# Row tiles and weight tiles loaded one by one at the start, and a new closing order, in a QKV projection on one core

## The chip, the cores and the metric

One core of a Trainium2 chip (trn2) runs the whole kernel. The metric is the device time of one execution in microseconds (us). A profiled execution has a **span**, from its first to its last recorded instruction, about 1.8 us shorter than that time.

## The reference, cut to what matters

```python
batch, seq, hidden = 16, 512, 768
x      # [16, 512, 768] float32
w_qkv  # [768, 2304]    float32

qkv = np.matmul(x, w_qkv)
q, k, v = qkv[..., :768], qkv[..., 768:1536], qkv[..., 1536:]
return np.stack([q, k, v], axis=0)
```

Flattened, x has 8192 rows, that is 64 row tiles of 128 rows or 32 pairs of row tiles.

## The kernel before

The first three pairs are multiplied plainly in bf16, against column blocks of 512, while the weights are still coming in. From pair 3 on a scheme with seven half-size products per pair is used. 256 "remainder" columns are always multiplied directly. A weight block of 512 columns comes as six k-tiles of 256 KB.

How row tiles are loaded, cast and turned (transposed by TensorE into PSUM, then copied out by the vector and scalar engines, half each):

```python
def load_rows(p):                       # one transfer for two row tiles, 768 KB
    xin[p] = xin_pool.tile([P, 2, K], fp32, name="xin")
    rows = x_flat[p * 2 * P:(p + 1) * 2 * P, :]
    nc.sync.dma_start(xin[p][:], rows.rearrange("(r m) k -> m r k", m=P))
# ... cast_rows(p): both tiles to bf16; turn_rows(p): six transposes each, copies
```

The order of the first loads, all on one queue, and of the first work:

```python
load_rows(0)
load_rows(1)
load_blocks(0, 0, 1)                    # six k-tiles, one transfer each
load_w(st_rem[:], 0, KT, R_OFF, REM)    # remainder columns
load_rows(2)
# ... more weights, more rows
busy(11)                                # filler matmuls on zeros
cast_rows(0); turn_rows(0)
busy(4)
cast_rows(1); cast_k(0); cast_k(1); turn_rows(1)
for j in range(2, KT): cast_k(j)
# ...
block(0, 0, b1[0], singles, nothing)    # four row tiles, k-tile by k-tile
rem(0); rem(1)                          # remainder columns of two pairs
cast_rows(2, False); turn_rows(2, False)
block(0, 0, b1[0], halves((4, 5)), nothing)
```

The closing order of the last pair (a and b are its two column halves, `do(u, n)` is product n with its eviction):

```python
do(a, 1); do(b, 1); do(a, 2); do(a, 6); do(b, 2); do(b, 6)
# ... stores, products 5 and 7
do(a, 4); rem_stored(0); do(b, 4)
do(a, 3); do(b, 3)
rem_stored(1)                           # remainder columns of the last row tile come last
```

## Time and profile before

| | before |
|---|---|
| time, median of the first 3 runs | 362.76 us |
| span of the profiled run | 361.4 us |
| TensorE busy | 353.3 us, 98% |
| first useful matmul | 9.19 us |
| first column block over six row tiles done | 20.54 us |
| last matmul to end of span | 4.53 us |

How to read it: the list of waits has no TensorE wait after 9 us, so only the start, the end and the work itself can move the time. The lines that carry this are in the prediction below.

### The profile page before, as it was taken

What the parts mean: (1) busy time and instruction counts of PE and PEld (TensorE: products, weight loads), DVE (VectorE), ACT (ScalarE), POOL (GpSimd) and SP (SyncE); (2) the same over time, 40 slices, a digit from 0 to 9 for tenths busy, and PEclk for the clock granted to TensorE, in tenths of its full rate; (3) what the DMA queues carried; (4) which work ended last, traced back from release to release, by engine and by line L of the source; (5) the groups of instructions that cost most, each with busy time, mean ns of one, the idle gap of its engine ahead of it and who ended that gap; (6) DMA issues with size and microseconds to landing.
All of it is one profiled execution on the core that took longest, in us unless ns stands there. A gap on an engine that the chain in (4) does not pass through costs nothing.

```text
span 361.4 us, 5220 instructions
## 1 busy us (share of the span) xinstructions
PE 353.3 (98%) x1765; PEld 250.8 (69%) x1797; DVE 222.7 (62%) x239; ACT 182.5 (51%) x304; POOL 174.4 (48%) x180
## 2 busy tenths in 40 slices
PE   8999999999999999999999999999999999999994
PEld 3644577777777777777777777777777777777763
DVE  3489546666566765566675565676556676556642
ACT  4547555455454545454545444445545454545452
POOL 0000970566664445664445665444666444566410
PEclk9999999999999999999999999999999999999999
DMA  7999969799899989999999999898999998989766
GB/s 294 381 383 338 348 227 345 271 354 304 279 322 298 296 275 296 282 313 314 284 278 295 282 306 316 284 276 291 295 285 317 295 296 276 297 279 331 267 251 242
DMA packets 80617, 108.08 MB, mean 299 GB/s; under 512 B 4816, under 2 KB 60368, under 8 KB 80592
## 3 DMA queue, kind: packets, MB, share of 16 engines
q1 hardware_dynamic: 65184, 96.35, 82.3%
q10 hardware_dynamic: 15408, 11.41, 9.9%
q8 instruction: 14, 0.23, 0.3%
q14 instruction: 11, 0.09, 0.1%
HBM read 32.24 MB, written 75.50 MB: 298 GB/s over the span
## 4 chain that ended last, share of the span: by engine, by line
PE 96%; ACT 1%; issue 1%; ACTq 0%; DVE 0%
PE ps L206 75%; PE ps L256 11%; PE ps L382 9%; PE ps L362 1%; PE ps L161 1%; ACT o L237 0%; ACTq L297 0%; ACT xb L141 0%; ACT orem L311 0%; DVE xb L139 0%; ACT xc L141 0%; ACTq L313 0%; DVE zero L340 0%; ACTq L311 0%
## 5 line engine op out<-in xcount | busy, mean ns | idle before, releaser
L206 PE MATMUL ps<-t,s 128*128 128x512 f32 x696 | 173.8, 398 | 0.0
L206 PEld LDWEIGHTS ps<-t,s 128*128 128x128 f32 x696 | 130.7, 188 | 29.8
L169 POOL CAST xb<-xf 128x1536 bf16<-128x1536 f32 x29 | 46.4, 1601 | 167.7 <-DVE xf L124 167.7
L234 DVE TENSOR_TENSOR o<-o,ps 128x512 f32<-128x512 f32 x58 | 39.9, 688 | 87.6 <-ACT o L233 87.6
L124 DVE STREAM_TRANSPOSE xf<-xin 128x1536 f32<-128x1536 f32 x29 | 85.7, 2956 | 9.7 <-DMA xin<-in_x_dram 7.1
L206 PE MATMUL ps<-b,xb 128*128 128x512 bf16 x320 | 82.4, 380 | 1.5
L233 ACT ACTIVATE o<-ps 128x512 f32<-128x512 f32 x58 | 34.7, 598 | 44.3 <-PE ps L206 44.3
L206 PEld LDWEIGHTS <-xb 128*128 128x128 bf16 x348 | 31.7, 98 | 35.6 <-issue 7.6
L227 ACT ACTIVATE o<-ps 128x512 f32<-128x512 f32 x58 | 34.8, 600 | 40.0 <-PE ps L206 37.3
L240 DVE TENSOR_TENSOR o<-o,ps 128x512 f32<-128x512 f32 x58 | 39.9, 688 | 21.4 <-PE ps L206 20.2
L206 PE MATMUL ps<-b,s 128*128 128x512 f32 x174 | 48.7, 389 | 0.0
L256 PE MATMUL ps<-w_rem,xb 128*128 128x256 bf16 x384 | 47.2, 273 | 0.0
L237 ACT ACTIVATE o<-ps 128x512 f32<-128x512 f32 x58 | 34.7, 598 | 24.1 <-PE ps L206 21.3
L220 ACT ACTIVATE o<-ps 128x512 f32<-128x512 f32 x58 | 34.6, 597 | 23.8 <-DVE o L240 20.7
L256 PEld LDWEIGHTS <-xb 128*128 128x128 bf16 x384 | 37.4, 98 | 11.2 <-issue 0.5
L224 DVE TENSOR_TENSOR o<-o,ps 128x512 f32<-128x512 f32 x58 | 36.5, 673 | 3.4 <-PE ps L206 2.1
L206 PEld LDWEIGHTS ps<-b,s 128*128 128x128 f32 x174 | 32.7, 188 | 6.8
L178 POOL TENSOR_TENSOR s<-s,xf 128x384 fp32r<-128x384 f32 x29 | 29.5, 1016 | 2.3
L266 ACT ACTIVATE orem<-ps 128x512 f32<-128x512 f32 x31 | 18.6, 598 | 22.7 <-PE ps L256 21.4
L179 POOL TENSOR_TENSOR s<-xf 128x384 fp32r<-128x384 f32 x29 | 29.5, 1017 | 0.0
L181 POOL TENSOR_TENSOR s<-xf,s 128x384 fp32r<-128x384 f32 x29 | 29.4, 1015 | 0.0
L177 POOL TENSOR_TENSOR s<-xf 128x384 fp32r<-128x384 f32 x29 | 29.3, 1012 | 0.0
(36 smaller groups left out, 127.2 us busy)
## 6 DMA issues: line engine op xcount, KB each, us to landing
out_dram<-o SPq DMA_DIRECT2D x62, 768.0 KB, 5.1
out_dram<-o SPq DMA_DIRECT2D x65, 256.0 KB, 4.6
xin<-in_x_dram SPq DMA_DIRECT2D x62, 192.0 KB, 6.7
xin<-in_x_dram ACTq DMA_DIRECT2D x54, 192.0 KB, 4.5
out_dram<-orem SPq DMA_DIRECT2D x31, 256.0 KB, 5.5
st<-in_w_qkv_dram SPq DMA_DIRECT2D x6, 768.0 KB, 14.1
xin<-in_x_dram SPq DMA_DIRECT2D x3, 768.0 KB, 5.8
st<-in_w_qkv_dram SPq DMA_DIRECT2D x6, 256.0 KB, 6.3
```

The source lines that it names most:

```text
L124: nc.vector.transpose(t[:].rearrange("p j (g b) -> p g j b", b=G), xin.pop(p)[:].rearrange("p g (a j) -> p g j a", a=G),)
L169: nc.gpsimd.tensor_copy(out=xb[p][:], in_=xf[p][:])
L206: nc.tensor.matmul(ps[:], lhs[j], rhs[j], start=(start and j == 0), stop=(j == KH - 1), skip_group_check=True,)
L220: nc.scalar.activation(c11, u.x[:], ident)
L224: nc.vector.tensor_tensor(c11, c11, u.z[:], op=add)
L227: nc.scalar.activation(c12, u.x[:], ident)
L233: nc.scalar.activation(c22, u.x[:], ident)
L234: nc.vector.tensor_tensor(c22, c22, u.y[:], op=add)
L237: nc.scalar.activation(c21, u.x[:], ident)
L240: nc.vector.tensor_tensor(c12, c12, u.y[:], op=add)
L256: nc.tensor.matmul(ps, xb[p][:, j, r * P:(r + 1) * P], w_rem[:, j, :], start=(j == 0), stop=(j == KT - 1), skip_group_check=True,)
L382: nc.tensor.matmul(ps[n][:], xb[p][:, j, r * P:(r + 1) * P], w[:, j, :], start=(j == 0), stop=(j == KT - 1), skip_group_check=True,)
```

## The change

Its intent is to start useful matmuls earlier and to shorten the end. The first loads come as row tiles 0, 1 and 2, k-tiles 0 to 4, row tile 3, k-tile 5; each row tile is a transfer of 384 KB. Three row tiles start on the k-tiles as they land, the fourth joins at the end. In the last pair the remainder columns go ahead of b's last two products, and the last eviction is cut in two halves.

```diff
-    def load_rows(p):
-        ...
-        nc.sync.dma_start(xin[p][:], rows.rearrange("(r m) k -> m r k", m=P))
+    def load_row(p, r):
+        if r == 0:
+            xin[p] = xin_pool.tile([P, 2, K], fp32, name="xin")
+        row = (2 * p + r) * P
+        nc.sync.dma_start(xin[p][:, r, :], x_flat[row:row + P, :])
 ... (cast_row and turn_row: likewise one tile at a time)
-    load_rows(0)
-    load_rows(1)
-    load_blocks(0, 0, 1)
+    load_row(0, 0)
+    load_row(0, 1)
+    load_row(1, 0)
+    for j in range(KT - 1):
+        load_k(j)
+    load_row(1, 1)
+    load_k(KT - 1)
 ... (remainder columns and pair 2: two transfers each in place of one)
-    busy(11)
-    cast_rows(0)
-    turn_rows(0)
-    busy(4)
-    cast_rows(1)
-    ...
+    busy(8)
+    cast_row(0, 0)
+    cast_row(0, 1)
+    turn_row(0, 0)
+    busy(1)
+    cast_row(1, 0)
+    turn_row(0, 1)
+    cast_k(0)
+    turn_row(1, 0)
 ... (block: k-tiles 0 to 4 for three tiles, fourth tile turned, k-tile 5, fourth tile)
-        do(a, 4); rem_stored(0); do(b, 4); do(a, 3); do(b, 3); rem_stored(1)
+        do(a, 4); do(a, 3); rem_stored(0); rem_stored(1); do(b, 4)
+        product(b, 3, b.y, False)        # evicted and stored in two halves of 256 columns
```

(The last two lines are condensed; the stores between them are left out.)

More of the change, by code (lines that the diff above doesn't have):

```diff
@@ L128, in transpose @@
         xf[p] = t
-    def load_rows(p):
-        xin[p] = xin_pool.tile([P, 2, K], fp32, name="xin")
-        rows = x_flat[p * 2 * P:(p + 1) * 2 * P, :]
-        nc.sync.dma_start(xin[p][:], rows.rearrange("(r m) k -> m r k", m=P))
+    def load_row(p, r):
[3 more added lines that the diff above has]
+        nc.sync.dma_start(xin[p][:, r, :], x_flat[row:row + P, :])
     def copy_halves(dst, src, two):
@@ L145, with cast_row, turn_row @@
     xc = {}
-    def cast_rows(p, two=True):
-        src = xin.pop(p)
-        xc[p] = s_pool.tile([P, 2, K], bf16, name="xc", tag="s")
-        for r in range(2):
-            halves = (slice(0, K // 2), slice(K // 2, K))
-            copy_halves([xc[p][:, r, n] for n in halves], [src[:, r, n] for n in halves], two)
-    def turn_rows(p, two=True):
-        c = xc.pop(p)
-        xb[p] = xb_pool.tile([P, KT, 2 * P], bf16, name="xb")
-        for r in range(2):
-            cols = c[:, r, :].rearrange("m (p j) -> m j p", j=KT)
-            ps = ps_pool.tile([P, KT, P], bf16, name="ps")
-            for j in range(KT):
-                nc.tensor.transpose(ps[:, j, :], cols[:, j, :], eye)
-            ks = (slice(0, KH), slice(KH, KT))
-            copy_halves(
-                [xb[p][:, n, r * P:(r + 1) * P] for n in ks], [ps[:, n, :] for n in ks], two
-            )
+    def cast_row(p, r, two=True):
+        if r == 0:
+            xc[p] = s_pool.tile([P, 2, K], bf16, name="xc", tag="s")
+        halves = (slice(0, K // 2), slice(K // 2, K))
+        copy_halves([xc[p][:, r, n] for n in halves], [xin[p][:, r, n] for n in halves], two)
+    def turn_row(p, r, two=True):
+        if r == 0:
+            xb[p] = xb_pool.tile([P, KT, 2 * P], bf16, name="xb")
+        cols = xc[p][:, r, :].rearrange("m (p j) -> m j p", j=KT)
+        ps = ps_pool.tile([P, KT, P], bf16, name="ps")
+        for j in range(KT):
+            nc.tensor.transpose(ps[:, j, :], cols[:, j, :], eye)
+        ks = (slice(0, KH), slice(KH, KT))
+        copy_halves(
+            [xb[p][:, n, r * P:(r + 1) * P] for n in ks], [ps[:, n, :] for n in ks], two
+        )
     def round_x(p):
@@ L313, in rem_stored @@
             nc.scalar.dma_start(out_flat[1, row:row + P, R_OFF - H:R_OFF - H + REM], o[:, 0, :])
-        do(a, 1)
-        do(b, 1)
-        do(a, 2)
-        do(a, 6)
-        do(b, 2)
-        do(b, 6)
+        for n in (1, 2):
+            for u in (a, b):
+                do(u, n)
         for u in (a, b):
             store_cols(u, 0, 0, CB, nc.sync)
-        for u in (a, b):
-            do(u, 5)
-            do(u, 7)
-            store_cols(u, 1, CB, 2 * CB, nc.sync)
+        do(a, 6)
+        do(a, 5)
+        do(b, 6)
+        do(a, 7)
+        store_cols(a, 1, CB, 2 * CB, nc.sync)
+        do(b, 5)
+        do(b, 7)
+        store_cols(b, 1, CB, 2 * CB, nc.sync)
         do(a, 4)
-        store_cols(a, 1, 0, CB, nc.scalar)
+        store_cols(a, 1, 0, CB, nc.sync)
+        do(a, 3)
+        store_cols(a, 0, CB, 2 * CB, nc.sync)
         rem_stored(0)
+        rem_stored(1)
         do(b, 4)
-        store_cols(b, 1, 0, CB, nc.scalar)
-        for u in (a, b):
-            do(u, 3)
-            store_cols(u, 0, CB, 2 * CB, nc.sync)
-        rem_stored(1)
+        store_cols(b, 1, 0, CB, nc.sync)
+        product(b, 3, b.y, False)
+        for lo in (CB, CB + CB // 2):
+            hi = lo + CB // 2
+            part = b.o[:, 0, lo:hi]
+            nc.vector.tensor_tensor(part, part, b.y[:, lo - CB:hi - CB], op=add)
+            store_cols(b, 0, lo, hi, nc.scalar)
     NS = 3
@@ L346, with load_k @@
     make_identity(nc, eye)
-    load_rows(1)
-    load_blocks(0, 0, 1)
-    st_rem = o_pool.tile([P, KT, REM], fp32, name="str", tag="o")
-    load_w(st_rem[:], 0, KT, R_OFF, REM)
-    load_rows(2)
-    load_blocks(0, 1)
+    st_0 = tq_pool.tile([P, KT, CB], fp32, name="st0", tag="tq")
+    stage[0, 0, 0], stage[0, 1, 0] = st_0[:, :KH, :], st_0[:, KH:, :]
+    def load_k(j):
+        load_w(st_0[:, j:j + 1], j, 1, Q_OFF[0], CB)
+    load_row(0, 1)
[4 more added lines that the diff above has]
+    load_k(KT - 1)
+    st_rem = o_pool.tile([P, KT, REM], fp32, name="str", tag="o")
+    for h in range(2):
+        load_w(st_rem[:, h * KH:(h + 1) * KH], h * KH, KH, R_OFF, REM)
+    for r in range(2):
+        load_row(2, r)
+    load_blocks(0, 1, KH)
     load_blocks(1, 0)
@@ L375, in block @@
         ps = {}
-        for js, tiles in groups:
+        for group in groups:
+            if callable(group):
+                group()
+                continue
+            js, tiles = group
             for n in tiles:
@@ L396, in halves @@
         return [(range(h * KH, (h + 1) * KH), tiles) for h in range(2)]
-    singles = [((0, ), (0, 1)), ((1, ), (0, 1)), ((0, 1), (2, 3))]
-    singles += [((j, ), range(4)) for j in range(2, KT)]
     act, dve = nc.scalar, nc.vector
-    def cast_k(j):
-        dve.tensor_copy(out=b1[0][:, j, :], in_=stage[0, j // KH, 0][:, j % KH, :])
     def cast_next(q, c, w):
@@ L412, with fourth_row @@
     nothing = lambda p: None
-    busy(11)
-    cast_rows(0)
-    turn_rows(0)
-    busy(4)
-    cast_rows(1)
+    busy(8)
[5 more added lines that the diff above has]
+    turn_row(0, 1)
     cast_k(0)
-    cast_k(1)
-    turn_rows(1)
-    for j in range(2, KT):
+    turn_row(1, 0)
+    for j in range(1, KT - 1):
         cast_k(j)
-    act.activation(w_rem[:, KH:], st_rem[:, KH:], ident)
-    dve.tensor_copy(out=w_rem[:, :KH], in_=st_rem[:, :KH])
+    def fourth_row():
+        cast_row(1, 1)
+        cast_k(KT - 1)
+        turn_row(1, 1)
+        for h in range(2):
+            ks = slice(h * KH, (h + 1) * KH)
+            dve.tensor_copy(out=w_rem[:, ks], in_=st_rem[:, ks])
     bt0 = bt_pool.tile([P, KT, CB], bf16, name="bt")
     bt1 = bt_pool.tile([P, KT, CB], bf16, name="bt")
-    block(0, 0, b1[0], singles, nothing)
-    rem(0)
-    rem(1)
-    cast_rows(2, False)
-    turn_rows(2, False)
-    block(0, 0, b1[0], halves((4, 5)), nothing)
+    block(
+        0, 0, b1[0],
+        [((j, ), range(3)) for j in range(KT - 1)]
+        + [fourth_row, ((KT - 1, ), range(3)), (range(KT), (3, ))],
+        nothing,
+    )
+    for p in range(2):
+        rem(p)
+        cast_row(2, p, False)
+        turn_row(2, p, False)
+    block(0, 0, b1[0], [(range(KT), (4, )), (range(KT), (5, ))], nothing)
     for h in range(2):
```

## The prediction

> **What bounds the kernel now.** I read the page's busy shares and chain first, then the timeline of the two ends, because only there can a change of loading order and of closing order matter. The page:
>
> ```profile
> PE 353.3 (98%) x1765; PEld 250.8 (69%) x1797; DVE 222.7 (62%) x239; ACT 182.5 (51%) x304; POOL 174.4 (48%) x180
> PE 96%; ACT 1%; issue 1%; ACTq 0%; DVE 0%
> ```
>
> TensorE is busy for 98% of the span and is 96% of the chain that ended last. The list of waits has no TensorE wait at all between 17 and 340 us. So the time is: when the gapless matmul stream can start, its length, and what follows its last matmul. The change touches no matmul of the long middle. The head, from the timeline's first 30 us (start us, duration us, engine, line, operation, count, wait):
>
> ```profile
> 1.19 4.88 PE L362 MATMUL ps<-zero 128*128 128x512 bf16 x11 [1.19 <-DVE zero L340]
> ...
> 8.40 0.95 PE L161 MATMUL ps<-eye,xc 128*128 128x128 bf16 x12 [0.57 <-ACT xc L141]
> 8.40 0.43 DVE L410 CAST b<-st 128x512 bf16<-128x512 f32 x1 [0.16 <-DMA st<-in_w_qkv_dram]
> ...
> 9.19 5.34 PE L382 MATMUL ps<-b,xb 128*128 128x512 bf16 x23
> ...
> 11.11 0.43 DVE L410 CAST b<-st 128x512 bf16<-128x512 f32 x1 [0.26 <-DMA st<-in_w_qkv_dram]
> 13.37 0.85 ACT L423 ACTIVATE w_rem<-str 128x768 bf16<-128x768 f32 x1 [3.10 <-DMA str<-in_w_qkv_dram]
> ```
>
> The first 9.2 us of TensorE are filler matmuls on zeros and transposes; useful matmuls begin at 9.19. The vector engine's waits date the landings: the last k-tile of weights at 11.1, the remainder columns at 13.4. The rest of the head, on TensorE alone:
>
> ```profile
> 14.37 2.78 PE L256 MATMUL ps<-w_rem,xb 128*128 128x256 bf16 x24
> 16.99 0.83 PE L161 MATMUL ps<-eye,xc 128*128 128x128 bf16 x12
> 17.94 2.76 PE L382 MATMUL ps<-b,xb 128*128 128x512 bf16 x11
> 20.54 7.93 PE L382 MATMUL ps<-bt,xb 128*128 128x512 bf16 x36
> ```
>
> The first column block over six row tiles ends at 20.54; from there TensorE never waits. **20.54 is the mark to beat.** The end:
>
> ```profile
> 355.56 1.37 DVE L240 TENSOR_TENSOR o<-o,ps 128x512 f32<-128x512 f32 x2 [1.42 <-PE ps L206]
> 356.04 0.55 PEld L256 LDWEIGHTS <-xb 128*128 128x128 bf16 x6 [0.26 <-issue]
> 356.04 0.83 PE L256 MATMUL ps<-w_rem,xb 128*128 128x256 bf16 x6
> 356.07 0.84 ACTq L297 DMA_DIRECT2D out_dram<-o  x2
> 357.01 0.38 ACT L311 ACTIVATE orem<-ps 128x256 f32<-128x256 f32 x1 [0.97 <-PE ps L256]
> 357.42 0.34 ACTq L313 DMA_DIRECT2D out_dram<-orem  x1
> ```
>
> TensorE ends at 356.04 + 0.83 = 356.87. The last two stores, remainder at 357.42 and b's last columns at 357.17 (the queue's timeline), take 2.2 and 2.5 us to land, so both at about 359.6. The span ends at 361.4: 4.53 us after TensorE, of which some 1.75 us after the last landing move nothing.
>
> **What the Trainium skill says.** "DMA: Bandwidth & Descriptors", section "Issuing engines are not separate DMA queues": transfers of all issuers run on the same 16 engines. The trace agrees: DMA share is 0.99 to 1.08 at 385 to 436 GB/s in each half microsecond from 4 to 10 us, so cutting loads smaller adds no bandwidth; only their order counts. "TensorE: Matmul & The Clock Gate", Part 1: the array starts at half clock and needs about 3.4 us of sustained work to reach full speed. The trace agrees: fillers start 0.43 us apart up to 5 us, and from 9.19 on 24 matmuls take about 0.215 us each. Part 4 there adds that transposes do not count as busy in the same way; the trace of before can't confirm that. "VectorE: DVE Perf Modes", section "Why PSUM operands drop a tier": an fp32 operation on PSUM runs at its slowest rate. It agrees: the add over 512 columns takes 688 ns, a cast of 512 columns from SBUF 420 ns.
>
> **The change part by part.**
> *Landings.* In before, k-tiles 1 to 5 land (by the casts that waited) at 8.38 and 11.09: 4 x 0.262 MB in 2.71 us, 0.387 MB/us. The first 0.786 MB (pair 0) land at 5.06. Both fit landing = 2.96 us + MB/0.387. Later ones come 0.25 us late of it: the remainder at 13.37, pair 2 at 15.43. The new order puts row tiles 0, 1, 2 (0.393 MB each) first, then k-tiles 0 to 4, row tile 3, k-tile 5. Estimates from the fit: rows 4.0, 5.0, 6.0; k0 6.7, k1 7.4, k2 8.0, k3 8.7, k4 9.4; row tile 3 10.4; k5 11.1; with the 0.25 us, remainder halves 12.4 and 13.4, rows of pair 2 14.4 and 15.4. Total bytes ahead of k5 and of pair 2 are unchanged, so these two don't land sooner.
> *Start.* The vector engine's order is now cast, cast, turn-copy 0, cast, turn-copy 1, k0, turn-copy 2. With about 0.32 us a cast and 0.37 us a copy from the trace: row 2's cast begins at 6.0, turn-copy 1 ends at 6.7, k0's cast at 7.1. So useful matmuls start near **7.2**, not 9.2. Three tiles per k-tile take 3 x 0.215 = 0.65 us, just what one k-tile takes to land (0.262/0.387 = 0.68). This part therefore runs at the transfers' pace: k4's matmuls end near 10.6. Row tile 3 is cast at 10.4 to 10.9, turned by 11.4; k5 is cast at 11.1 to 11.52. Then k5 for three tiles and all of tile 3: 9 x 0.215 = 1.94 us, from 11.57 to **13.5**. In before the four tiles end at 14.5. So of 2 us earlier start about 1 us survives; the remainder is eaten by waiting for k5.
> *Behind it.* Remainder pair 0 (12 x 0.109 = 1.31 us) runs at 13.5, but its second half's cast ends near 13.95, some 0.15 us of gap, to 15.0; transposes of row 4 (0.35 us; its two casts end near 15.05) to 15.4; remainder pair 1 to 16.7; row 5 cast at 16.1 to 16.7, transposes to 17.1; tiles 4 and 5, 12 x 0.215, to **19.75**. Before: 20.54. Head gain: **0.8 us**, an estimate; with no gaps at all it would be 1.2 us.
> *Middle.* Nothing downstream comes sooner (the next weight half is cast at 20.87 as its load lands), but nothing is due either: that cast ends at 21.8 and TensorE would want it at 19.75 + 3.9 = 23.6. For pair 3, xb is ready at 41.4 and wanted at 45.2; for pair 5 I put the slack at 2.7 us. So 0.8 us should pass through to the end.
> *Tail.* The same 42 + 12 matmuls. Last is now product 3 of b, not the remainder. Its eviction is two adds over 256 columns. Casts of 384 and 1536 columns take 0.35 and 0.95 us, so about 0.15 us of an operation is fixed; half of 0.688 - 0.15, plus 0.15, is 0.42 us each. The second half is ready 0.06 + 0.84 = 0.9 us after TensorE's end, is issued at about 1.0, and lands after some 2.0 us (the 128 KB stores of before: 1.7 to 2.3): 3.0 us, against 2.8 (359.6 - 356.87) now. But the end of before had 256 KB more queued in its last 1.7 us. Tail: **0.2 us longer**, estimate, between -0.2 and +0.4.
> Sum: -0.8 + 0.2 = **-0.6 us**.
>
> **The rivals.**
> 1. *The clock.* Only 8 fillers, ending near 1.19 + 8 x 0.427 = 4.6, precede transposes with gaps; in before 11 fillers plus 4 more. If full clock comes only at about 9.6, matmuls at half clock (1.28 us per k-tile) fall behind the loads: k0 and k1 would take until 9.6, k5 end 0.2 to 0.6 us later. If it came only at 13, the loss is over 2 us and the change would be slower by about 1.5 us. For it: fewer fillers, and the skill on transposes. Against: useful matmuls start 2 us earlier and are themselves dense. I give it 30% for the mild form, 8% for the severe one.
> 2. *The head gain is hidden anyway.* Were the pairs of the middle bound by loads (DMA share 0.94 from 70 to 340 us), starting early would only end in a wait. Against: no TensorE wait in the middle. Time then 362.9; 7%.
> 3. *The tail is transfers.* 339 to 373 GB/s move from 357 to 359 us, so the closing stores are a backlog. Sending row 0's columns of a and the remainders earlier leaves 512 KB for the last microsecond instead of 0.9 MB; if bandwidth set the end, the tail shortens by up to 0.5 us and the total gain is 1.3 us: 361.5. Against: landings of 2.2 to 2.5 us are near those of an idle moment. 15%.
>
> **Range and chances.** The measured time lies 1.4 us above the span of the profile; I carry that over. 362.76 - 0.6 = 362.2, shaded by rival 1 within rounding. Rival 3 with a gapless head gives 361.5 as the lower end; a mild slow clock plus a longer tail gives about 362.9 as the upper end. Two per cent would be 7.3 us; the whole head before 9.2 and the whole tail of 4.5 hold no such gain, and no rival loses that much. So faster 0.01, same 0.98, slower 0.01.
>
> **What would show it.** Right: first useful matmul near 7.2; k5's cast still waiting for its load at about 11.1; first block done near 19.75 in place of 20.54; TensorE without waits from there on; its end near 356.1; 4.7 us from there to the end of the span. Wrong: matmuls 0.43 us apart after 7.2 (clock); a TensorE wait between 20 and 70 us (gain given back); row tiles landing later than the fit, if smaller loads move slower; a tail under 4.3 us (backlog).

## The result, and the profile after

| | before | after |
|---|---|---|
| time, median of 6 runs | 362.74 us | 363.92 us |
| range | 362.67 to 363.44 | 363.28 to 364.33 |
| span of the profiled run | 361.4 us | 362.2 us |
| first useful matmul | 9.19 us | 8.13 us |
| last k-tile landed, by the cast that waited | 11.1 us | 12.1 us |
| first column block done | 20.54 us | 21.29 us |
| last matmul to end of span | 4.53 us | 4.58 us |

The ratio of the times is 1.0029, 95% interval 1.0016 to 1.0042: slower by a third of a per cent, clear of noise. A ratio is the mean time of one kernel's fast runs over that of the other's of the same rounds, so not quite the ratio of the medians quoted.

The page of the changed kernel, busy shares and the chain that ended last:

```profile
PE 354.7 (98%) x1791; PEld 250.3 (69%) x1791; DVE 225.9 (62%) x241; ACT 182.4 (50%) x303; POOL 173.8 (48%) x180
PE 96%; DMA 2%; SPq 0%; DVE 0%; DVEq 0%; issue 0%
```

Still bound by TensorE. New is the DMA's 2%: the chain now starts with a load. TensorE's timeline of the changed kernel:

```profile
1.19 3.58 PE L380 MATMUL ps<-zero 128*128 128x512 bf16 x8 [1.19 <-DVE zero L345]
...
7.53 0.54 PE L160 MATMUL ps<-eye,xc 128*128 128x128 bf16 x6 [1.55 <-ACT xc L142]
8.13 5.02 PE L405 MATMUL ps<-b,xb 128*128 128x512 bf16 x15
12.99 0.50 PE L160 MATMUL ps<-eye,xc 128*128 128x128 bf16 x6
13.32 2.11 PE L405 MATMUL ps<-b,xb 128*128 128x512 bf16 x9
...
18.70 2.75 PE L405 MATMUL ps<-b,xb 128*128 128x512 bf16 x12
21.29 7.93 PE L405 MATMUL ps<-bt,xb 128*128 128x512 bf16 x36
```

Two things stand out. TensorE idles 1.55 us before the transposes of row tile 2. And 15 matmuls take 5.02 us, 0.33 us each, where the nine after them take 2.11. The vector engine's timeline dates the landings:

```profile
4.86 0.36 DVE L140 CAST xc<-xin 128x384 bf16<-128x384 f32 x1 [0.74 <-DMA xin<-in_x_dram]
...
6.95 0.36 DVE L140 CAST xc<-xin 128x384 bf16<-128x384 f32 x1 [1.45 <-DMA xin<-in_x_dram]
...
12.12 0.43 DVE L426 CAST b<-st 128x512 bf16<-128x512 f32 x1 [0.37 <-DMA st<-in_w_qkv_dram]
```

Row tile 1 lands at 4.86, row tile 2 only at 6.95, 2.1 us behind it for 384 KB, and the last k-tile at 12.12. The windows show why. Columns: window, its length, TensorE busy (count), granted clock, DMA share, GB/s. First the kernel before, then the changed one:

```profile
4.00:5.00 1.00, 1.00 (x3) 1.00 1.01 406
5.00:6.00 1.00, 1.00 (x5) 1.00 1.03 418
```

```profile
4.00:5.00 1.00, 1.00 (x9) 1.00 1.05 323
5.00:6.00 1.00, 0.85 (x9) 1.00 0.94 258
6.00:7.00 1.00, 0.00 (x0) 1.00 0.94 353
```

The clock column reads 1.00 wherever the trace has no clock record yet; the first is at 6.4 us in before and at 4.6 us in after.

The transfer engines are about as busy (share 0.94 to 1.05) but move 20% and then 38% less. Their single packets show the rest. In the kernel before, between 3.3 and 9 us, no packet of 2 or 3 KB takes over 0.19 us; the median is 0.084 and 0.121 us. In the changed kernel ten take over 0.4 us, the longest 1.28 us. Summing what each took beyond the median gives 10.4 us, **0.65 us for each of 16 engines on average**, against 0.05 us before. I call this average the **stall** below and give it for every run (worked out from the packet records of the traces; to line the runs up, times are shifted so that the first data packet, at about 1.8 us of the span, stands at 2.2 us).

The average hides that the delay is uneven. The trace shows 16 semaphore increments for each of these loads, and a load has landed with its last. For the last k-tile they come between 10.53 and 11.09 us before, between 10.75 and 12.10 us after: the first is 0.2 us later, the last 1.0 us. I call the time from first to last the **spread**; the table below has it beside the stall. The dependent work waits for the last of the 16.

The other new thing is the clock (columns as before, here with all engines: busy of PE, PEld, DVE, ACT, POOL, then clock, DMA share, GB/s):

```profile
4.60:8.00 3.40, 1.73 (x20) 1.20 (x19) 1.61 (x5) 1.93 (x4) 0.00 (x0) 1.00 0.97 335
8.00:11.40 3.40, 3.33 (x10) 1.13 (x8) 2.15 (x7) 0.60 (x3) 0.00 (x0) 0.50 1.04 390
```

TensorE was busy for half of one stretch of 3.4 us, and its clock was halved in the next. Three of the six runs show this lapse in their mean clock (0.992, mean time 364.19 us); the other three (0.999 and 1.000) average 363.56. So the lapse goes with some 0.6 us (three runs against three), and the others are still behind. That those three had no loss by the clock is not shown: the mean counts only from the first clock record on, so a clock that opens late leaves no mark in it (alternate below has a mean of 0.997, but its first record of a full clock is at 13.9 us).

The end, last matmuls, split eviction and last stores:

```profile
356.76 0.86 PE L205 MATMUL ps<-b,s 128*128 128x512 f32 x3
...
357.66 0.75 DVE L339 TENSOR_TENSOR o<-o,ps 128x256 f32<-128x256 f32 x2 [2.04 <-PE ps L205]
358.11 0.82 ACTq L296 DMA_DIRECT2D out_dram<-o  x2
```

From 357.62 to the span's end are 4.58 us. The end is neutral.

### The profile page after: what moved, and what is told of

Same layout as the page of the kernel before. It is cut to its first block, busy times and chain, and to the rows that moved or that the text cites. A ratio compares the mean times of both kernels' runs of the same rounds, so it can differ in the third digit from the quotient of the medians.

```text
span 362.2 us, 5247 instructions
## 1 busy us (share of the span) xinstructions
PE 354.7 (98%) x1791; PEld 250.3 (69%) x1791; DVE 225.9 (62%) x241; ACT 182.4 (50%) x303; POOL 173.8 (48%) x180
## 4 chain that ended last, share of the span: by engine, by line
PE 96%; DMA 2%; SPq 0%; DVE 0%; DVEq 0%; issue 0%
PE ps L205 76%; PE ps L255 12%; PE ps L405 9%; DMA st<-in_w_qkv_dram 2%; SPq L136 0%; PE ps L160 0%; DVE b L426 0%; DVE o L339 0%; DVEq L521 0%
## 5 line engine op out<-in xcount | busy, mean ns | idle before, releaser
L168 POOL CAST xb<-xf 128x1536 bf16<-128x1536 f32 x29 | 43.9, 1512 | 169.0 <-DVE xf L124 169.0
L205 PE MATMUL ps<-b,xb 128*128 128x512 bf16 x348 | 84.7, 380 | 0.0
L176 POOL TENSOR_TENSOR s<-xf 128x384 fp32r<-128x384 f32 x29 | 30.9, 1064 | 0.0
L178 POOL TENSOR_TENSOR s<-xf 128x384 fp32r<-128x384 f32 x29 | 29.4, 1014 | 0.0
```

The lines of the kernel that those rows point to most:

```text
L168: nc.gpsimd.tensor_copy(out=xb[p][:], in_=xf[p][:])
L205: nc.tensor.matmul(ps[:], lhs[j], rhs[j], start=(start and j == 0), stop=(j == KH - 1), skip_group_check=True,)
```

## The experiments

**My theory after the result**: the loss lies in the head. Loading the first two row tiles as two transfers makes the transfer engines stall, everything lands about 1 us late, and TensorE's clock sometimes lapses on top. **Rivals**: the closing order costs the time; the clock alone does; the stalls come from something else (casts beside the loads, the order of loads, any short transfer).

All runs, with stall and spread as defined above and the landing of the last k-tile ("k5", by the cast that waited; "up to" where it did not wait). Stall, spread and landings are those of the one execution that was profiled:

| run | time, median us (runs) | ratio to before | stall us per engine | k5's spread us | k5 us | first block done us |
|---|---|---|---|---|---|---|
| before | 362.74 (6) | | 0.05 | 0.56 | 11.1 | 20.54 |
| after | 363.92 (6) | 1.0029 | 0.65 | 1.35 | 12.1 | 21.29 |
| head_only | 363.65 (6) | 1.0018 | 0.68 | 1.13 | 11.9 | 21.19 |
| tail_only | 362.94 (5) | 1.0000 | 0.06 | 0.54 | 11.1 | 20.37 |
| fill6 | 363.80 (5) | 1.0021 | 0.96 | 1.47 | 12.4 | 21.19 |
| pair0 | 363.05 (5) | 1.0005 | 0.07 | 0.44 | 11.1 | 20.42 |
| before_split0 | 364.29 (4) | 1.0041 | 0.92 | 2.19 | 13.2 | 22.26 |
| k_between | 365.50 (1) | | 0.58 | 1.15 | 11.9 | 22.67 |
| late_cast | 364.11 (1) | | 0.80 | 0.99 | 12.0 | 21.39 |
| cand1 | 362.90 (5) | 1.0002 | 0.12 | 0.77 | 11.3 | 20.11 |
| before_split1 | 363.06 (1) | | 0.17 | 1.10 | 11.5 | 20.51 |
| before_k0first | 363.48 (1) | | 0.07 | 0.52 | up to 11.0 | 20.85 |
| row1_actq | 363.34 (4) | 1.0019 | 0.14 | 0.46 | 11.0 | 19.70 |
| three_one | 363.44 (5) | 1.0014 | 0.08 | 0.58 | up to 11.3 | 20.97 |
| col_split0 | 364.08 (4) | 1.0030 | 0.14 | 1.32 | 12.1 | 21.10 |
| even_odd0 | 363.67 (4) | 1.0028 | 0.26 | 0.76 | 11.3 | 20.24 |
| alternate | 365.94 (4) | 1.0077 | 0.72 | 0.99 | 12.0 | 23.21 |

Runs with a single execution (k_between, late_cast, before_split1, before_k0first): I use their landings and stalls, not their times. How far one profile can be trusted: after, head_only, fill6 and late_cast share their first loads and all stall (0.65 to 0.96); before and tail_only share theirs and neither does (0.05 and 0.06; first block done at 20.54 and 20.37, so differences of 0.2 us in the last column say nothing).

### Which end? head_only and tail_only

head_only is the changed kernel with the old closing order; tail_only is the old kernel with the new one.

```diff
 # tail_only: the kernel before, its closing order replaced by the changed one
-        do(a, 6); do(b, 2); do(b, 6); ...; do(a, 3); do(b, 3); rem_stored(1)
+        do(b, 2); do(a, 6); ...; do(a, 3); rem_stored(0); rem_stored(1); do(b, 4); ...
```

> The changed head with the old closing order. Theory (the loss is in the head: TensorE idles near 6 to 7.5 us waiting for row tile 2, its clock halves for one 3.4 us window, and the single-k-tile matmuls then run at 0.43 us): time as the changed kernel, 363.3 to 364.3 us, first column block ending near 21.3 us where the clock lapses. Rival (the closing order costs the time): 362.2 to 362.7 us.

> The old head with the changed closing order. Theory (head): within 0.2 us of the kernel before, 362.7 to 362.9 us, 4.6 us from TensorE's end to the span's end as against 4.53. Rival (closing order costs): 363.3 us or more.

tail_only is level with before (1.0000, interval 0.9988 to 1.0012). head_only carries a loss (1.0018, 1.0001 to 1.0035) with the same stall and the same lapse; its three runs at a clock of 0.995 or less average 364.17 us, the other three 363.15, only 0.2 us over the mean of before in the same rounds (362.98). The rival of the closing order is out.

### The clock? fill6

```diff
     turn_row(0, 1)
     cast_k(0)
+    busy(6)
     turn_row(1, 0)
```

> The changed kernel with six more filler matmuls between the transposes of row tiles 1 and 2, where TensorE idled 1.55 us. Theory (clock): no stretch at half clock, k-tiles at 0.65 us, k5's cast at 12.1 us then the bound, first block ends near 20.4 us, time near 362.6 us, and all runs alike. Rival (late landings alone cost the time, the clock is hidden behind them): no change, 363.5 to 364 us.

TensorE's and the vector engine's timelines of fill6:

```profile
5.89 1.46 PE L380 MATMUL ps<-zero 128*128 128x512 bf16 x6
7.92 0.54 PE L160 MATMUL ps<-eye,xc 128*128 128x128 bf16 x6 [0.57 <-ACT xc L142]
8.52 3.47 PE L405 MATMUL ps<-b,xb 128*128 128x512 bf16 x15
```

```profile
12.43 0.43 DVE L426 CAST b<-st 128x512 bf16<-128x512 f32 x1 [0.36 <-DMA st<-in_w_qkv_dram]
```

The lapse is gone: the 15 matmuls take 3.47 us in place of 5.02, and no run has a mean clock under 0.996. Yet the first block ends at 21.19 and the time is 363.8. The expectation of 362.6 failed: with the clock held, the late landings are the bound (in the profiled run k5 came even 0.3 us later than after). So the clock alone is not the cause; it can be a second cost beside the loads.

### The split of the first load? pair0 and before_split0

pair0 is the changed kernel with row tiles 0 and 1 in one transfer. before_split0 is the opposite: the kernel before with nothing changed but its first load.

```diff
 # before_split0
+        if p == 0:
+            for r in range(2):
+                nc.sync.dma_start(xin[p][:, r, :], rows[r * P:(r + 1) * P, :])
+            return
         nc.sync.dma_start(xin[p][:], rows.rearrange("(r m) k -> m r k", m=P))
```

> The changed kernel with row tiles 0 and 1 loaded as one transfer, as in the kernel before, and row tile 2 behind it. Theory A (splitting rows into three loads made packets slow between 4.5 and 6.3 us): row tile 2 lands near 6.0 to 6.2 us in place of 6.95, k5 near 11.2 to 11.4 in place of 12.1, the idle stretch shrinks, time 362.5 to 363. Theory B (the slow packets have nothing to do with the split): row tile 2 again near 7 us, time 363.5 to 364.

> The kernel before, with nothing changed but that its first load of two row tiles is issued as two loads of one row tile each. Theory A (single row tiles at the very start make later transfers stall): packets of up to about 1 us between 4.5 and 6.5 us, and the last k-tile landing near 11.8 to 12.4 us in place of 11.1, time 363.2 to 363.8 us. Theory C (it takes three single rows, or the rest of the new order): last k-tile at 11.1 us, time as before.

The vector engine's cast of the last k-tile, in pair0 and then in before_split0:

```profile
11.14 0.43 DVE L431 CAST b<-st 128x512 bf16<-128x512 f32 x1 [0.33 <-DMA st<-in_w_qkv_dram]
```

```profile
13.21 0.43 DVE L414 CAST b<-st 128x512 bf16<-128x512 f32 x1 [0.25 <-DMA st<-in_w_qkv_dram]
```

With the pair whole the stall is gone, k5 is back at 11.1, and the time (363.05, a little over the 362.5 to 363 expected) is level with before: 1.0005, interval 0.9993 to 1.0017. With only the pair cut, the unchanged rest of the kernel before loses 2.1 us of landing and 1.4 us of time (364.29 against 362.89 us in the same rounds), more than theory A had expected; TensorE then waits in front of the second pair's transposes:

```profile
9.73 0.95 PE L165 MATMUL ps<-eye,xc 128*128 128x128 bf16 x12 [2.61 <-ACT xc L145]
```

So the split of the first load by itself is enough to cause a loss, and undoing it is enough to remove the changed kernel's (though no gain is left either).

### Something beside the loads? late_cast and k_between

late_cast holds the first casts back with dummy copies (nine on the vector engine, five on the scalar engine), so that no engine reads the row tiles before about 5.2 us. k_between loads k-tiles 0 and 1 ahead of row tile 2.

```diff
 # late_cast
+    for _ in range(9):
+        dve.tensor_copy(out=t_0[:, 0, 0, :], in_=zero[:])
+    for _ in range(5):
+        act.activation(t_0[:, 3, 0, :], zero[:], ident)
     busy(8)
 # k_between
     load_row(0, 1)
+    load_k(0)
+    load_k(1)
     load_row(1, 0)
```

> The changed kernel with dummy copies on the vector and scalar engines that hold the first casts back until about 5 us; the loads are untouched. Theory A (the loads alone stall): slow packets between 4.5 and 6.5 us stay, row tile 2 lands near 7 us, k5 at about 12. Rival (casts and transposes that read the row tiles while loads still write disturb the loads): no slow packets, row tile 2 near 6 us, k5 near 11.1.

> The changed kernel with k-tiles 0 and 1 loaded ahead of row tile 2. Theory A (the two single row loads at the start): transfers stall between 4.5 and 6.5 us again, though k-tiles move there, k5 lands at 11.8 to 12.4 us. Theory D (row tile 2 as the third row load in a line is what stalls): no stall, k5 at 11.1 us.

Both stall as the changed kernel does (0.80 and 0.58 us per engine). In late_cast row tile 2 is cast at 6.87 and k5 at 12.04, although nothing had read a row tile while the stalls began. Casts and transposes beside the loads are out, and so is row tile 2 as the culprit.

### Any short transfer, and where? before_split1, before_k0first, row1_actq, three_one

before_split1 cuts the second pair's load instead of the first. before_k0first puts k-tile 0 (256 KB) ahead of everything and leaves both pairs whole. row1_actq is the changed kernel with row tile 1 issued from the scalar engine's queue. three_one loads row tiles 0 to 2 as one transfer (with 12 fillers ahead in place of 8).

```diff
 # row1_actq
-        nc.sync.dma_start(xin[p][:, r, :], x_flat[row:row + P, :])
+        eng = nc.scalar if (p, r) == (0, 1) else nc.sync
+        eng.dma_start(xin[p][:, r, :], x_flat[row:row + P, :])
 # three_one
+                nc.sync.dma_start(three, x_flat[:3 * P, :].rearrange("(r m) k -> m r k", m=P))
```

> The kernel before with its second load of two row tiles issued as two loads, the first left whole. Theory (only a short transfer at the very start makes the queue stall): no stall, last k-tile lands at 11.1 us, time as before, 362.7 to 363.4. Rival (any single row tile load between 2 and 8 us stalls): last k-tile at 11.8 us or later, time 363.3 or more.

> The kernel before with k-tile 0 (256 KB) loaded ahead of everything, both pairs of row tiles whole. Theory (any short first transfer makes later ones stall): packets of 0.5 us and more between 4 and 8 us, last k-tile lands at 11.8 us or later. Rival (it is the two single row tiles in a line that stall): no stall, last k-tile at 11.1 us, rows of pair 0 at 5.7 us in place of 5.1.

> The changed kernel with row tile 1 issued from the scalar engine's queue instead of the sync engine's, so two queues share the transfer engines from the start. If the stalls come from one queue working through short transfers back to back: no stalls, row tile 2 near 6.0 us, k5 near 11.1 us, time 362.2 to 362.8. If they come from the short row transfers whatever queue issues them: k5 at 11.8 to 12.4 us again, time 363.3 to 364.2.

> The changed kernel with row tiles 0, 1 and 2 in one transfer and 12 fillers ahead in place of 8, so that TensorE is not idle until they land. Theory (the stalls follow the short first transfers): no slow packets after 3.5 us, the three tiles land near 6.1 us, k5 near 11.1 us, first block done near 20.1 us, time 362.5 to 363.0. Rival (the order of loads itself, not their size, delays them): row tiles near 7 us, k5 near 12 us, time 363.5 or more.

before_split1 is a mild case that fits neither side: stall 0.17, spread 1.10, k5 at 11.47. before_k0first does not stall at all (0.07), so my theory that any short first transfer does it fell: what stalls is the pair cut into two. three_one doesn't stall either, but its three tiles are first cast at 6.26, useful matmuls start at 9.14, the first block ends at 20.97 (20.1 was expected), and the time is 363.44 (362.5 to 363.0 expected): no gain that way.

row1_actq is the most telling profile. TensorE and the vector engine:

```profile
7.79 3.70 PE L406 MATMUL ps<-b,xb 128*128 128x512 bf16 x15
...
19.70 1.46 PE L406 MATMUL ps<-bt,xb 128*128 128x512 bf16 x6
```

```profile
10.96 0.43 DVE L427 CAST b<-st 128x512 bf16<-128x512 f32 x1 [0.35 <-DMA st<-in_w_qkv_dram]
```

Here row tile 2 (5.8 us) and k5 come as predicted, and the first block ends at 19.70, where the prediction had 19.75. The start is still late, 7.79 in place of 7.2: row tile 1, on the other queue, lands only at 5.96. But the four runs are 362.42, 362.64, 364.03 and 365.44 us: two ahead of before's median of 362.82, two far behind. Only the fastest was profiled, so I can't show that the slow two stalled. As a version it is inconclusive (1.0019, interval 0.9989 to 1.0049).

### An attempt to keep the gain: cand1

pair0's loads, ten fillers, no filler between the transposes, and k-tile 0 multiplied for tiles 0 and 1 before row tile 2 is turned.

```diff
-        [((j, ), range(3)) for j in range(KT - 1)]
+        [((0, ), range(2)), third_row, ((1, ), range(2)), ((0, 1), (2, ))]
+        + [((j, ), range(3)) for j in range(2, KT - 1)]
```

> An attempt to keep the gain: row tiles 0 and 1 in one transfer, no filler between their transposes, ten fillers ahead, and k-tile 0 multiplied for tiles 0 and 1 before row tile 2 is turned. If late landings and idle TensorE were the whole loss: first useful matmul near 7.8 us, no lapse of the clock, k5 landing at 11.1 us, first block done near 19.8 us, time 362.0 to 362.5 us. Rival (the head is bound by landings in any order): 362.7 us or more.

The first useful matmul is at 7.63, the clock holds, k5 is at 11.3, and the first block ends at 20.11: 0.3 to 0.4 us better than in the profiles of tail_only and before. The time is the same (1.0002, interval 0.9988 to 1.0016), so the 362.0 to 362.5 expected failed. A gain of 0.4 us is smaller than what these runs resolve. No version was faster than the kernel before, clear of noise.

### What about the two row tiles? col_split0, even_odd0, alternate

All three were made to settle what in the cut first load stalls. col_split0 cuts it by columns, even_odd0 into even and odd rows, alternate is the changed kernel with rows and k-tiles taking turns.

```diff
 # col_split0
+            for n in (slice(0, K // 2), slice(K // 2, K)):
+                nc.sync.dma_start(xin[p][:, :, n], both[:, :, n])
 # even_odd0
+            spread = rows.rearrange("(m r) k -> m r k", r=2)
+                nc.sync.dma_start(xin[p][:, r, :], spread[:, r, :])
 # alternate
+    load_k(0)
     load_row(0, 1)
+    load_k(1)
     load_row(1, 0)
```

> The kernel before with its first load of two row tiles issued as two loads of half the columns each, so both transfers are 384 KB but each covers both row tiles with 1.5 KB pieces. Theory E (two transfers of that size in a line at the start stall, whatever they read): k5 at 11.8 us or later, time 363.3 or more. Theory F (it is the reading of one row tile after the other, 384 KB in one contiguous stretch each, that stalls): no stall, k5 near 11.1 us, time as before.

> The kernel before with its first load issued as two single-tile loads, the first taking the even and the second the odd rows of the first 256 (wrong result on purpose: rows of the first pair come out permuted). Pieces stay 3 KB and 128 to a transfer, but neither transfer is one contiguous stretch. Theory F (contiguous stretch): no stall, k5 near 11.1 us, time as before. Theory E (two transfers of 128 pieces at the start): k5 at 12 to 13.3 us, time 363.5 or more, as when the pair was split by tiles.

> The changed kernel with loads in the order row 0, k0, row 1, k1, row 2, k2 and on, so that no two row tiles follow each other. Theory G (two row tiles in a line stall): no stalls, k5 near 11.1 us, row 2 near 7.3 us, time 362.5 to 363.2 if the clock holds. Rival (row tiles loaded singly stall wherever they stand at the start): k5 at 11.8 us or later, time 363.5 or more.

alternate has the largest ratio of all (1.0077) and stalls (0.72), so the two row tiles needn't follow each other. Its stall is about that of after; the rest of its loss goes with row tile 2, cast at 8.29 behind two k-tiles, and with the clock, which is not full before 13.9 us (15 matmuls take 5.56 us). In the profiled runs of the other two few packets are slow (0.14 and 0.26), but that does not clear them. In col_split0 fifteen of k5's sixteen increments have come by 11.30 us and the last comes at 12.04, and the last is as far behind in every load from the second pair on: in this profile the loss is one late share, which the average of the stall hides. So theory F, the contiguous stretch, failed there: k5 is at 12.1, and the time is 0.3% longer. even_odd0 is 0.3% slower too, but the profiled run was its fastest (362.76, others up to 364.64), so its trace says little. Shown is that cutting the first load costs time in all three ways tried (by tile, by column, by even and odd rows). **What inside the transfer path stalls is left open.**

## Why the prediction was wrong, point by point

- **The bound** was read rightly: TensorE is 96% of the chain after as before, and it has no wait after the head. The windows from 70 to 340 us show 270.00 us busy.
- **The step that failed** is *Landings*, and the sentence it rests on: that "cutting loads smaller adds no bandwidth; only their order counts". The number beside that sentence (DMA share near 1 from 4 to 10 us; its lowest is 0.98, not 0.99) shows one queue keeping the engines busy with the transfers of before; it says nothing of transfers cut differently. The fit of landing time to bytes was carried over to those all the same. Row tile 2 came at 6.95 in place of 6.0, k5 at 12.1 in place of 11.1. The queue was not just a pipe of 0.387 MB/us: with the pair cut, packets stalled, 0.65 us per engine on average and more on the slowest share, for which each landing waits. before_split0 shows this in isolation (0.92 us, k5 at 13.2).
- **Start** at 7.2 became 8.13, and the first block 21.29 in place of 19.75. The first block's working held where the landings came on time: in row1_actq it was 19.70. There the start was 7.79, so the agreement shows that the block hangs on k5 and what follows it, not on the start.
- **Rival 1, the clock**, was put at 38%. A lapse shows in half of the runs and goes with 0.6 us, the upper end of its mild form, but not in the form given: the rival had full clock come late, and in the profile it came at 4.6 us and was lost from 8.0 to 11.4, after TensorE had idled because row tile 2 was late. fill6 shows that curing the clock doesn't cure the time.
- **Rival 2** (gain hidden in the middle) never came into play: no wait appeared there. **Rival 3** (closing stores as a backlog) is out: tail_only is level.
- **Tail**: +0.2 us was expected, +0.05 measured, because the kernel before was misread. The prediction gave its last store 2.2 us and put the landing at 359.6; by the landing records that store took 2.6 us, to 360.04, which is 3.17 us after TensorE's end and not 2.8. In after the last store lands 3.21 us after TensorE's end, not 3.0: the two half adds are shorter than expected (0.75 us together, not 0.84), the landing longer (2.3 us, not 2.0).
- **Sum**: -0.8 + 0.2 was expected. The profiles give +0.75 for the head and +0.05 for the tail, 0.8 us in span. A smaller slip: I carried over 1.4 us from span to time, but the profiled run of before was itself a slow one of its kind (363.17 us), so the difference is 1.8 us.
- The chances (98% within 2%) were right; the range, which allowed no loss beyond 0.14 us, was too narrow because a stall of the queue was not among the rivals.

## What to carry to other kernels

A landing time fitted to one cutting of the loads is not valid for another: test the cut alone (one line here) before building a schedule on it. When a start depends on a load, look at the GB/s, the slowest packets and the spread of the landings in the first microseconds, not at the DMA share, which stays near 1 while the engines stall. A TensorE that waits a microsecond and a half in the first ten can pay a second time through its clock.

## What the Trainium skill lacked or had wrong

- "DMA: Bandwidth & Descriptors", section "Rules for kernel authors", asks for 1 MiB or more per transfer for best bandwidth. It has no warning about the first transfers: cutting a 768 KB load into two of 384 KB delayed the landing of the last k-tile, seven transfers on, from 11.1 to 13.2 us, while k-tiles of 256 KB ran at 387 to 404 GB/s in the kernel before (7 to 9 us), and a 256 KB transfer ahead of whole pairs did not delay the loads (last k-tile by 11.0 us). Size alone isn't the rule.
- The same page, section "Issuing engines are not separate DMA queues", says that a second issuing queue saves only issue time. In row1_actq one transfer on the other queue went with a stall of 0.14 us in place of 0.65 in the one profile; its times (362.42 to 365.44) leave open whether that holds.
- "TensorE: Matmul & The Clock Gate", Part 1, gives the idle window of about 3.4 us after which the clock halves. The trace agrees on the length (half clock from 8.0 to 11.4 us). But the window before it was not idle: TensorE was busy 1.73 of 3.40 us, part of it transposes. The page does not say how much work keeps the clock up. In the first 20 us of the 17 profiles here the clock was lost after windows of 3.41 us with TensorE busy for 1.49 to 1.77 us (after, head_only, k_between, late_cast), and held after windows with 2.02 us (three_one) or more; but at the end of head_only it was held after one with 1.47 us, so busy time alone gives no clean threshold.
